# Input products of a recurrent layer: the seven-product scheme over 14 instead of 12 of 16 K tiles, with another plan for the weight sums and another order of products

## The chip, the cores and the metric

One core of one Trainium2 chip. The time is the device time of one launch in microseconds (us). TensorE multiplies; VectorE, ScalarE and GpSimd work elementwise; SyncE only issues DMAs here. In profiles they are PE (and PEld, its weight loads), DVE, ACT, POOL and SP.

## What is computed

The reference is one step of a two-layer trunk over 640 tokens of width 2048: 512 tokens of a prompt and 8 sequences of 16 tokens. The first layer is recurrent, the second is attention. The part that the change touches is the input side of the recurrent layer:

```python
def recurrent_mixer(hn, h0, conv0, w_in, conv_w, conv_b, w_r, b_r, w_i, b_i, lam, w_out):
    xb, zg = jnp.split(hn @ w_in, 2, axis=-1)
    xb, conv_new = causal_conv(xb, conv0, conv_w, conv_b)
    y, hT = rg_lru(xb, h0, w_r, b_r, w_i, b_i, lam)
    return (y * jax.nn.silu(zg)) @ w_out, hT, conv_new
```

`hn` is the normed input (640 x 2048), `w_in` is 2048 x 8192. Half of the 8192 outputs are features `xb`, half are gates `zg`. `rg_lru` makes two sigmoid gates from `xb` by small block products, then exp, tanh and sqrt, and scans over the tokens.

## The kernel before

**Layout.** Features lie on partitions, tokens along the free axis. The inner dimension of 2048 is 16 K tiles of 128, the outputs are 64 feature tiles of 128, and the 640 tokens are two halves of 320. Everything is float32 by way of three matmuls: operands are split into a high part in float32r and a low rest, and `mm3` (L99) adds high by high, high by low and low by high. So a weight tile that came by DMA is split first: `hilo` (L82) writes the high part on ScalarE (L87, tile wh) and the rest on VectorE (L88, tile wl).

**The stages.** A start stage norms the input, makes the conditioning vectors and already does the first four feature tiles (two of `xb`, two of `zg`, the list EARLY). The recurrent stage does the other 60 feature tiles as 30 pairs. Then come the output product of the layer, the shared keys and values, attention and its output product.

**A pair product** (`pair_product`, L543) makes two feature tiles for both halves of the tokens: a 2x2 block of results. For 12 of the 16 K tiles, taken as NP = 6 pairs, it uses a scheme that needs seven products instead of eight: sums of the input halves (the slots X11, X12, X22, S1 to S4 of the tiles xs) are made once in the start stage (`combine`, L403), and sums of weight quarters are made per pair of feature tiles. Each product is NP x 3 matmuls of 128x128 by 128x320. The other four K tiles (PLAIN, tiles xv) are done directly. Four banks hold partial results: a, b, c and d (pa, pb, pc, pd). Between products ScalarE copies bank a or c to SBUF (`keep`, L567), and VectorE combines a bank with a kept copy into the result (the evac functions, L637 and L682). TensorE goes on adding into the bank after the copy has read it, so a product that goes on in a bank waits for that bank's keep.

**The weights of a pair** come in nine slots, one for each of the seven products and two plain ones. `plan` (L441) and `pair_weights` (L499) are generators that write the loads, sums and splits in a fixed order; `ahead` (L535) keeps up to WB = 4 split slots ready. A sum of weight quarters is built by DMA: SyncE loads one quarter into a tile (`big_load`, L477), and GpSimd issues a second DMA which adds another quarter to it (`add`, L481). Six tiles rotate: r11 and r2 hold raw quarters, t1, t2, t3 and u2 hold sums. Each pair takes six loads and five additions of 384 KB, and two plain loads of 256 KB.

**Order around the products.** For `j` from 0 to 15 the recurrent stage does `silu_gates` (a pair product for `zg`, its evac into tiles zs, a sigmoid sg of it), `lru` (L691: gate blocks psg of 48 matmuls, their sigmoids g and q, then exp, tanh and sqrt on ScalarE, the scan on VectorE, and the results to DRAM tensor yd), and `inputs` and `conv` for the next pair of `xb`. ScalarE loads another function table ahead of the first sigmoid, the first exp and the first sqrt of each `j`. The scheduler of the tile framework sets the order on each engine from this program; each engine then works in order, and an instruction that waits holds up what stands behind it. `conv_rows` (L601) prepares the row buffers hb of the convolution: a memset and a copy of three columns per sequence (L609, L610), on GpSimd, after a small load pv.

In a steady period, from one gate block to the next, TensorE does 48 gate matmuls and two pair products of 174, in all 396.

## Time and profile before

| | |
|---|---|
| median of 3 runs | 2928.18 us (2927.59 to 2935.82) |
| the profiled execution | 2928.68 us |
| its span in the trace | 2927.0 us |
| TensorE busy | 2845.4 us, 97% |
| VectorE / ScalarE / GpSimd busy | 67% / 55% / 15% |
| start stage | 0 to about 144 us |
| recurrent stage, first to last pair product | about 144 to 1049 us |
| loads and additions of w_in_a quarters, median from issue to landing | 5.3 us (r), 3.6 us (t) / 6.4 us (t) |

The span is the time from the first to the last recorded instruction; the rest of the execution's time lies around it. In the rows of the timeline, columns are start in us, duration in us, engine, line, operation, output and inputs, shape and count; in brackets stands the idle time ahead of it and what ended it. In the groups, a row gives the count, the total busy time, the mean of one in ns, and after the second bar the idle time ahead of them. A matmul's duration includes its way through the array; matmuls that follow each other start about 147 ns apart while one lasts about 309 ns.

### The profile page before, as it was taken

Reading aid. Unit: us, or ns where it says so; the run is one execution under the profiler, and the core shown is the slowest. Engines: PE = TensorE matmul, PEld = TensorE weight load, DVE = VectorE, ACT = ScalarE, POOL = GpSimd, SP = SyncE. Lnnn points to the kernel's source line nnn. Section 1 sums busy time; section 2 is a strip of 40 time slices with the busy share of each in tenths; the row PEclk is TensorE's granted clock in tenths of the full one; section 3 lists DMA queues with packets and bytes.
Section 4 is the critical chain, followed back from the end, with each engine's and each line's share of the span. In section 5 each row is a group of like instructions: output and inputs, shape, how many; then the busy total and the mean of one; then the engine's idle time right before and its main releaser. Section 6 shows DMA issues by size and latency. Waiting matters only on the chain.

```text
span 2927.0 us, 48683 instructions
## 1 busy us (share of the span) xinstructions
PE 2845.4 (97%) x18874; PEld 2532.5 (87%) x18874; DVE 1961.7 (67%) x2795; ACT 1608.0 (55%) x2459; POOL 437.5 (15%) x683
## 2 busy tenths in 40 slices
PE   6889999999999999999999999999999999999998
PEld 4689999999999987778878999878989999897787
DVE  7666776677667766724468877787666766667335
ACT  5456655665566556623456667674455555546323
POOL 0022222223222200001113332001100000001000
PEclk9999999999999999999999999999999999999999
DMA  9977787778777756555567666663665555656636
GB/s 333 330 164 167 184 194 195 177 182 195 191 183 181 170 163 211 171 138 171 176 223 259 217 212 215 206 195 111 193 192 171 181 176 181 200 169 190 209 106 225
DMA packets 263287, 564.07 MB, mean 193 GB/s; under 512 B 24440, under 2 KB 108536, under 8 KB 261904
## 3 DMA queue, kind: packets, MB, share of 16 engines
q1 hardware_dynamic: 232016, 465.60, 50.1%
q0 software_dynamic: 31040, 95.36, 15.7%
q8 instruction: 148, 2.42, 0.3%
q14 instruction: 83, 0.68, 0.1%
HBM read 523.76 MB, written 37.11 MB: 192 GB/s over the span
## 4 chain that ended last, share of the span: by engine, by line
PE 85%; DMA 6%; ACT 4%; DVE 4%; issue 1%; POOL 0%; SPq 0%; DVEq 0%; POOLq 0%; ACTq 0%
PE acc L101 7%; PE acc L102 7%; PE acc L103 7%; PE psh L101 6%; PE acck L101 5%; PE psh L103 5%; PE psh L102 5%; PE acck L102 5%; PE acck L103 5%; PE pa L101 3%; PE pa L102 3%; PE pa L103 3%; PE pc L102 2%; PE pc L103 2%; PE pc L101 2%; DMA wa<-w_ada_dram 2%
## 5 line engine op out<-in xcount | busy, mean ns | idle before, releaser
L88 DVE TENSOR_TENSOR wl<-wr,wh 128x1024 fp32r<-128x1024 f32 x216 | 270.5, 1254 | 285.4 <-ACT wh L87 282.2
L87 ACT ACTIVATE wh<-wr 128x1024 fp32r<-128x1024 f32 x216 | 228.1, 1056 | 379.6 <-PE acc L103 221.7
L101 PE MATMUL acc<-wh,yh 128*128 128x512 f32 x960 | 379.4, 396 | 9.8 <-ACT yh L785 5.4
L102 PE MATMUL acc<-wl,yh 128*128 128x512 f32 x960 | 378.0, 394 | 5.7 <-DVE wl L88 5.6
L103 PE MATMUL acc<-wh,yl 128*128 128x512 f32 x960 | 375.3, 393 | 0.8 <-DVE yl L786 0.8
L186 DVE TENSOR_TENSOR wa<-wa,wa 128x1024 bf16<-128x1024 f32 (+1 forms) x256 | 313.6, 1260 | 23.0 <-ACT wa L185 20.9
L101 PE MATMUL psh<-nh,wh 128*128 128x320 f32 x1024 | 323.9, 316 | 0.0
L103 PE MATMUL psh<-nh,wl 128*128 128x320 f32 x1024 | 318.8, 311 | 0.0
L102 PE MATMUL psh<-nl,wh 128*128 128x320 f32 x1024 | 317.4, 310 | 0.0
L185 ACT ACTIVATE wa<-wa 128x1024 bf16<-128x1024 f32 x256 | 263.6, 1052 | 67.5 <-DVE wa L186 52.8
L101 PEld LDWEIGHTS acc<-wh,yh 128*128 128x128 f32 x960 | 182.1, 190 | 58.1 <-issue 8.7
L102 PEld LDWEIGHTS acc<-wl,yh 128*128 128x128 f32 x960 | 182.3, 190 | 45.7 <-DVE wl L88 8.4
L103 PEld LDWEIGHTS acc<-wh,yl 128*128 128x128 f32 x960 | 182.0, 190 | 39.8 <-DVE yl L786 2.1
L101 PEld LDWEIGHTS psh<-nh,wh 128*128 128x128 f32 x1024 | 192.3, 188 | 19.3 <-DVE ql L1120 12.6
L103 PEld LDWEIGHTS psh<-nh,wl 128*128 128x128 f32 x1024 | 192.4, 188 | 0.5 <-DVE wl L88 0.2
L102 PEld LDWEIGHTS psh<-nl,wh 128*128 128x128 f32 x1024 | 192.4, 188 | 0.1
L101 PE MATMUL pa<-xs,wh 128*128 128x320 f32 x540 | 171.8, 318 | 19.7 <-ACT keep L567 14.2
L481 POOL DMA_DIRECT2D t<-w_in_a_dram x105 | 93.5, 891 | 622.6 <-DMA t<-w_in_a_dram 465.1
L102 PE MATMUL pa<-xs,wh 128*128 128x320 f32 x540 | 168.3, 312 | 0.0
L103 PE MATMUL pa<-xs,wl 128*128 128x320 f32 x540 | 168.1, 311 | 0.0
L101 PE MATMUL acck<-nh,wh 128*128 128x320 f32 x512 | 161.5, 315 | 0.0
L103 PE MATMUL acck<-nh,wl 128*128 128x320 f32 x512 | 158.2, 309 | 0.0
(353 smaller groups left out, 7436.5 us busy)
## 6 DMA issues: line engine op xcount, KB each, us to landing
wa<-w_ada_dram SPq DMA_DIRECT2D x192, 512.0 KB, 4.7
wr<-w_out_a_dram SPq DMA_DIRECT2D x96, 512.0 KB, 4.3
t<-w_in_a_dram POOLq DMA_DIRECT2D x105, 384.0 KB, 6.4
r<-w_in_a_dram SPq DMA_DIRECT2D x90, 384.0 KB, 5.3
wr<-w_in_b_dram SPq DMA_DIRECT2D x64, 512.0 KB, 5.4
ck<-cache_k_dram SPq DMA_DIRECT2D x64, 512.0 KB, 6.5
cv<-cache_v_dram SPq DMA_DIRECT2D x64, 512.0 KB, 5.3
t<-w_in_a_dram SPq DMA_DIRECT2D x75, 384.0 KB, 3.6
```

The lines of the kernel that those rows point to most:

```text
L87: nc.scalar.activation(hi[:, :n], raw, AF.Copy)
L88: nc.vector.tensor_tensor(lo[:, :n], raw, hi[:, :n].bitcast(F32), ALU.subtract)
L101: mm(out, sh, mh, start=start, stop=False, **kw)
L102: mm(out, sh, ml, start=False, stop=False, **kw)
L103: mm(out, sl, mh, start=False, stop=stop, **kw)
L185: nc.scalar.activation(parts[i], raw, AF.Copy)
L186: nc.vector.tensor_tensor(parts[2] if i else raw, raw, parts[i], ALU.subtract)
L481: self.nc.gpsimd.dma_start(self.big[tag], self.quarter(w, i), accum_op=ALU.add)
```

## The change

- **NP goes from 6 to 7.** A product has 21 matmuls instead of 18, the plain part has two K tiles instead of four: 147 + 24 = 171 matmuls for a pair instead of 174. Split tiles are 128x896 instead of 128x768, plain slots 128x256 instead of 128x512.
- **The weight sums are chains.** A sum tile (sum0 and sum1 in turn) serves three slots of a pair: it is split, a quarter is added, it is split again, another is added, it is split a third time. Beside it are raw (two slots, plain loads), rest (a load, and an addition between its two slots) and one plain load for both plain slots. That makes four loads and four additions of 448 KB and one load of 256 KB for a pair. In the start stage one addition falls away, and the tiles that the early weights borrow are others.
- **Another order of products.** Before: X11, S1, S2, X12, plain b, S3, X22, plain d, S4, plain c, plain a. Now: S1, X11, S4, plain b and d, S2, X12, S3, plain c and a, X22. The copy of S1 gets a buffer of its own (keep5), the others have two instead of three. The result of bank a is taken before X22, that of bank d is the last.
- **The ring of split weights** has three buffers instead of four.
- **The row buffers** are prepared by VectorE instead of GpSimd.
- In the start stage there is a seventh pair to combine, and the input tiles are divided among other buffers.

```diff
--- before.py
+++ after.py
@@ -34,7 +34,7 @@
 NHEAD = 16
 PAST = 512
-NP = 6
+NP = 7
 PLAIN = range(2 * NP, KD)
 WQ = NP * P
@@ -300,7 +300,7 @@
         V.memset(self.ones, 1.0)
         acc = rp.tile([P, T], F32, tag="row", name="ssum", bufs=4)
-        homes = [("A", 7, (0, 1, 2, 3, 4, 5)), ("A", 7, (6, 7)), ("A", 7, (8, 9)), ("V", 2, (10, 12)), ("V", 2, (11, 13)), ("V", 2, (14,)), ("V", 2, (15,))]
+        homes = [("A", 7, (0, 1, 2, 3, 4, 5)), ("A", 7, (6, 7)), ("A", 7, (8, 9)), ("A", 7, (10, 11)), ("V", 2, (12, 14)), ("V", 2, (13, 15))]
         xs = [None] * KD
         for tag, n, ks in homes:
             x = self.ap.tile([P, n, T], F32, tag=tag, name=f"x{tag}", bufs=self.ABUFS[tag])
@@ -346,7 +346,7 @@
         spare = [self.zeroed(self.bank(n)) for n in ("psb", "pss")]
         units, wt = [], {}
-        tags = [t for t in self.BIG if t not in ("t2", "u2")]
+        tags = ("rest", 1), ("raw", 1), ("rv", 3), ("rv", 3)
         self.big = {}
         def fill(k):
@@ -362,9 +362,9 @@
                 with self.tc.issue_after(last):
                     r = self.spread(rp, rs)
             if k == 9:
-                self.big_load("t2", self.I["w_in_a"][1], 2)
-            if k in (11, 13):
-                self.add("t2", self.I["w_in_a"][1], (13 - k) // 2)
+                self.big_load("sum0", self.I["w_in_a"][1], 1)
+            if k == 11:
+                self.add("sum0", self.I["w_in_a"][1], 0)
             if k < 2 * NP:
                 if k % 2 == 0:
                     slot = self.ap.tile([P, 2, 7 * HALF], F32R, tag="A", name="xs", bufs=self.ABUFS["A"])
@@ -389,7 +389,8 @@
                     if k == 1:
                         units = self.first_units()
                     fill(k - 1)
-            raw = self.wp.tile([P, WQ], F32, tag=tags[(k - KD) % len(tags)], name="wf", bufs=1)[:, :512]
+            tag, bufs = tags[(k - KD) % len(tags)]
+            raw = self.wp.tile([P, 512 if tag == "rv" else WQ], F32, tag=tag, name="wf", bufs=bufs)[:, :512]
             nc.sync.dma_start(raw, self.I["w_first"][:, 4 * P * k : 4 * P * k + 4 * P])
             wt[k] = self.hilo(raw, P)
             if k % 2 == 0:
@@ -444,7 +445,7 @@
         order = [1] + [q for j in range(1, 16) for q in (16 + j, j + 1)][:-1]
         small = []
         for q in order:
-            small += [(w[q][:, 4 * WQ + i : 4 * WQ + i + WV], None) for i in (0, WV)]
+            small.append((w[q][:, 4 * WQ : 4 * WQ + 2 * WV], None))
             if q == 1 or q > 16:
                 small += [(x[0, max(0, q - 16)].rearrange("(k p) n -> p k n", p=P), 256) for x in g]
         self.small = iter(small)
@@ -452,19 +453,18 @@
         for _ in range(3):
             self.small_load()
         at = [w[q] for q in order] + [None, None]
-        for tag, n in (("r11", 0), ("t1", 1), ("r2", 3), ("t3", 1), ("u2", 2)):
-            self.big_load(tag, at[tag == "u2"], n)
-        for tag, n in (("t1", 0), ("t3", 2), ("u2", 1)):
-            self.add(tag, at[tag == "u2"], n)
+        for tag, n in (("raw", 0), ("rest", 2), ("sum1", 1)):
+            self.big_load(tag, at[tag == "sum1"], n)
         for i, q in enumerate(order):
-            yield from self.pair_weights(*at[i : i + 3], *("t2", "u2", "t2")[i % 2 : i % 2 + 2])
+            yield from self.pair_weights(*at[i : i + 3], *("sum0", "sum1", "sum0")[i % 2 : i % 2 + 2])
             if q == 1 or q > 16:
                 for _ in g:
-                    yield self.small_split(256)
-    BIG = "r11", "t1", "t2", "r2", "t3", "u2"
+                    x = self.urgent(self.smalls.pop(0), 256)
+                    self.small_load()
+                    yield x
     def quarter(self, w, i):
         return w[:, WQ * i : WQ * i + WQ]
@@ -472,7 +472,7 @@
     def big_load(self, tag, w, i):
         if w is not None:
-            pool = self.ep if tag == "u2" else self.wp
+            pool = self.ep if tag == "sum1" else self.wp
             self.big[tag] = pool.tile([P, WQ], F32, tag=tag, name=tag, bufs=1)
             self.nc.sync.dma_start(self.big[tag], self.quarter(w, i))
@@ -483,7 +483,7 @@
     def small_load(self):
         for src, width in islice(self.small, 1):
             raw = self.wp.tile([P, 512], F32, tag="rv", name="rv", bufs=3)
-            n = WV if width is None else 512
+            n = 2 * WV if width is None else 512
             self.nc.sync.dma_start(raw[:, :n] if width is None else raw.rearrange("p (a n) -> p a n", n=width), src)
             self.smalls.append(raw[:, :n])
@@ -491,45 +491,39 @@
         with self.tc.high_priority(200):
             return self.hilo(raw, width)
-    def small_split(self, width):
-        x = self.urgent(self.smalls.pop(0), width)
-        self.small_load()
-        return x
-    def pair_weights(self, w, after, later, t2, other):
+    def pair_weights(self, w, after, later, total, other):
         load, add = self.big_load, self.add
         split = lambda tag: self.urgent(self.big[tag], P)
-        x = split("r11")
-        load("r11", after, 0)
+        x = split(total)
+        add(total, w, 2)
         yield x
-        x = split("t1")
-        load("t1", after, 1)
+        x = split("raw")
+        load("raw", w, 3)
         yield x
-        x = split(t2)
-        add(t2, w, 3)
+        x = split("rest")
+        add("rest", w, 1)
         yield x
-        x = split("r2")
-        load("r2", w, 2)
-        add("t1", after, 0)
-        yield x
-        x = self.small_split(P)
+        plain = self.smalls.pop(0)
+        x = self.urgent(plain[:, :WV], P)
         add(other, after, 0)
         yield x
-        x = split("t3")
-        load("t3", after, 1)
+        x = split(total)
+        add(total, w, 3)
         yield x
-        x = split(t2)
-        load(t2, later, 2)
+        x = split("raw")
+        load("raw", after, 0)
         yield x
-        x = split("r2")
-        load("r2", after, 3)
-        add("t3", after, 2)
+        x = split("rest")
+        load("rest", after, 2)
         yield x
-        x = self.small_split(P)
-        add(t2, later, 1)
+        x = self.urgent(plain[:, WV:], P)
+        self.small_load()
+        yield x
+        x = split(total)
+        load(total, later, 1)
         yield x
     def ahead(self, held=0):
@@ -556,58 +550,56 @@
                 self.mm3(ps, hi[:, n, :], lo[:, n, :], x[:, 0, c], x[:, 1, c], first and n == 0, n == NP - 1, **kw)
             self.ahead()
-        def plain(ps, w, half):
+        def plain(ps, w, half, first):
             c = slice(HALF * half, HALF * half + HALF)
             for n, k in enumerate(PLAIN):
                 mh, ml = self.hT[k]
-                self.mm3(ps, w[0][:, n, :], w[1][:, n, :], mh[:, c], ml[:, c], False, k == KD - 1, **kw)
-        def keep(ps):
-            t = ep.tile([P, HALF], F32, tag="keep", name="keep", bufs=3)
+                self.mm3(ps, w[0][:, n, :], w[1][:, n, :], mh[:, c], ml[:, c], first and n == 0, k == KD - 1, **kw)
+        def keep(ps, tag="keep", bufs=2):
+            t = ep.tile([P, HALF], F32, tag=tag, name=tag, bufs=bufs)
             nc.scalar.activation(t, ps, AF.Copy)
             return t
-        a, c = bank("pa7"), bank("pc7")
+        c, a = bank("pc7"), bank("pa7")
+        seven(c, S1, True)
+        p5 = keep(c, "keep5", 1)
         seven(a, X11, True)
         p1 = keep(a)
-        seven(c, S1, True)
-        p5 = keep(c)
+        seven(c, S4, False)
+        b, d = bank("pb7"), bank("pd7")
+        w = self.weights()
+        plain(b, w, 0, True)
+        plain(d, w, 1, True)
+        self.ahead()
         seven(a, S2, False)
         u2 = keep(a)
-        b = bank("pb7")
-        seven(b, X12, True)
-        w = self.weights()
-        plain(b, w, 0)
+        seven(b, X12, False)
         evac(0, 0, b, p1, ALU.subtract)
-        d = bank("pd7")
-        plain_d = lambda: plain(d, w, 1)
         seven(a, S3, False)
         u3 = keep(a)
-        seven(d, X22, True)
-        plain_d()
-        self.ahead()
-        evac(0, 1, d, u3, ALU.subtract)
-        seven(c, S4, False)
         w = self.weights()
-        plain(c, w, 0)
+        plain(c, w, 0, False)
         evac(1, 0, c, u2, ALU.add)
-        plain(a, w, 1)
+        plain(a, w, 1, False)
         self.ahead()
         evac(1, 1, a, p5, ALU.add)
+        seven(d, X22, False)
+        evac(0, 1, d, u3, ALU.subtract)
     HW = 3 + TP + NB * (TS + 3)
     S0 = 3 + TP
     def conv_rows(self, j, ep):
-        G = self.nc.gpsimd
+        V = self.nc.vector
         pv = ep.tile([P, 2, 40], F32, tag="pv", name="pv", bufs=2)
         self.nc.sync.dma_start(pv, self.I["lru"][:, 2 * j : 2 * j + 2, :])
         rows = []
         for h in range(2):
             hb = ep.tile([P, self.HW + 1], F32, tag="hb", name="hb", bufs=2)
-            G.memset(hb[:, 0:3], 0.0)
-            G.tensor_copy(hb[:, self.S0 : self.HW].rearrange("p (b t) -> p b t", t=TS + 3)[:, :, 0:3], pv[:, h, 8:32].rearrange("p (b t) -> p b t", t=3))
+            V.memset(hb[:, 0:3], 0.0)
+            V.tensor_copy(hb[:, self.S0 : self.HW].rearrange("p (b t) -> p b t", t=TS + 3)[:, :, 0:3], pv[:, h, 8:32].rearrange("p (b t) -> p b t", t=3))
             rows.append(hb)
         return pv, rows
@@ -1371,7 +1363,7 @@
             self.od = dp.tile([D, T], F32, name="od")
             self.constants()
             self.pp = E(self.pool("ps", space=PSUM))
-            self.WB, self.WW = 4, WQ
+            self.WB, self.WW = 3, WQ
             with self.pool("A") as self.ap, self.pool("w7") as self.wp:
                 self.h0t = self.mp.tile([P, NB], F32, name="h0t")
                 self.k4, self.nk8 = (self.mp.tile([P, FT], F32, name=n) for n in ("k4", "nk8"))
```

What the scheduler makes of it is seen in the order of instructions on an engine. On GpSimd, from the end of the start stage to the first convolution, there stood before (t and u are tiles of weight sums, hb the row buffers, st the states for the output):

```order
L481 DMA t_1548<-w_in_a_dram 128x768
L609 MEMSET hb 128x3 x2
L652 COPY st<-hb 128x3
L653 COPY st<-hb 128x24
L652 COPY st<-hb 128x3
L653 COPY st<-hb 128x24
L481 DMA u_1533<-w_in_a_dram 128x768
L610 COPY hb<-pv 128x8x3 x2
L481 DMA u_1533<-w_in_a_dram 128x768
```

Now there stands:

```order
L481 DMA rest<-w_in_a_dram 128x896
L644 COPY st<-hb 128x3
L645 COPY st<-hb 128x24
L644 COPY st<-hb 128x3
L645 COPY st<-hb 128x24
L481 DMA sum_1543<-w_in_a_dram 128x896
L481 DMA sum_952<-w_in_a_dram 128x896
```

The copies into hb have gone from between two additions to VectorE's queue.

On ScalarE, at a gate block in the middle of the stage (sg is the sigmoid of a pair product's result, g and q the gates), before:

```order
L687 ACT_TABLE_LOAD
L687 ACTIVATE sg<-zs 128x640
L87 ACTIVATE wh<-r_5194 128x768
L87 ACTIVATE wh<-t_5220 128x768
L687 ACTIVATE sg<-zs 128x640
L710 ACTIVATE g<-psg_5576,pv 128x320
L710 ACTIVATE g<-psg_5584,pv 128x320
L710 ACTIVATE q<-psg_5593,pv 128x320
```

and now:

```order
L87 ACTIVATE wh<-sum_5742 128x896
L679 ACT_TABLE_LOAD
L679 ACTIVATE sg<-zs 128x640
L702 ACTIVATE g<-psg_6096,pv 128x320
L702 ACTIVATE g<-psg_6104,pv 128x320
L702 ACTIVATE q<-psg_6113,pv 128x320
L679 ACTIVATE sg<-zs 128x640
L702 ACTIVATE q<-psg_6121,pv 128x320
```

Before, the table load and the first sg stood two weight splits ahead of the gates; now a weight split stands ahead of the table load, and the gates follow right behind the first sg.

Also on ScalarE, from the exp of a period to the second product of the next pair, before:

```order
L720 ACT_TABLE_LOAD
L720 ACTIVATE q<-g,nk_100 128x640
L87 ACTIVATE wh<-rv 128x512
L720 ACTIVATE q<-g,nk_100 128x640
L724 ACTIVATE g<-g,k_99 128x640 x2
L87 ACTIVATE wh<-t_4713 128x768
L732 ACT_TABLE_LOAD
L732 ACTIVATE g<-g 128x640
L87 ACTIVATE wh<-t_4461 128x768
L732 ACTIVATE g<-g 128x640
L567 ACTIVATE keep<-pa_5044 128x320
L738 ACTIVATE q<-q,mone 128x640
```

and now:

```order
L712 ACT_TABLE_LOAD
L712 ACTIVATE q<-g,nk_100 128x640
L87 ACTIVATE wh<-rv 128x256
L712 ACTIVATE q<-g,nk_100 128x640
L716 ACTIVATE g<-g,k_99 128x640 x2
L561 ACTIVATE keep_5611<-pc_5583 128x320
L87 ACTIVATE wh<-sum_5102 128x896
L724 ACT_TABLE_LOAD
L724 ACTIVATE g<-g 128x640 x2
L87 ACTIVATE wh<-raw 128x896
L730 ACTIVATE q<-q,mone 128x640
L87 ACTIVATE wh<-rest 128x896
```

The first keep (of bank c, keep5) stands now behind tanh instead of the first keep (of bank a) behind sqrt, and the split of the raw quarter (for X12) stands behind both sqrt.

On TensorE the scheduler also moves some matmuls: in the first pair product after a gate block, three plain matmuls of bank b stand between X11 and S4, and X12 begins ahead of S2.

## The prediction

> **What bounds the kernel now.** I read the page first.
>
> ```profile
> PE 2845.4 (97%) x18874; PEld 2532.5 (87%) x18874; DVE 1961.7 (67%) x2795; ACT 1608.0 (55%) x2459; POOL 437.5 (15%) x683
> ```
>
> TensorE is busy for 97% of the span, so time is to be won in two ways only: fewer matmuls, or less waiting of TensorE. The recurrent stage is the one that the change touches, so I cut it with the table of windows where the start-up of that stage ends and the steady periods begin (columns: length, busy time of PE, PEld, DVE, ACT, POOL, the granted clock, the DMA share, GB/s).
>
> ```profile
> 144.00:282.00 138.00, 123.64 (x793) 121.50 (x794) 92.19 (x148) 77.43 (x122) 30.95 (x64) 0.95 0.71 169
> 282.00:1049.00 767.00, 761.54 (x5150) 754.93 (x5149) 551.28 (x831) 463.24 (x688) 182.99 (x316) 1.00 0.75 181
> ```
>
> The steady part has 5150 matmuls, 13 periods of 396, so a period is 767 / 13 = 59.0 us. The first part loses 14 us of TensorE, and its granted clock is lower. Next come the waits of TensorE in the whole stage, and then in its steady part alone (engine, tile, line, what it waited for: sum, times, longest).
>
> ```profile
> PE pa L101 <- ACT keep L567: 18.1, 17, 6.2
> PE pa L101 <- ACT hb L632: 5.5, 1, 5.5
> ```
>
> ```profile
> PE pa L101 <- ACT keep L567: 5.0, 13, 0.4
> ```
>
> So in the steady part TensorE waits once a period, 0.4 us, for a keep; the rest, 13.1 + 5.5 us, is lost in the first 138 us. The timeline of TensorE there shows two of these waits and what follows them.
>
> ```profile
> 138.44 0.28 PE L103 MATMUL pss<-xv,wl 128*128 128x256 f32 x1
> 144.22 0.64 PE L101 MATMUL pa<-xs,wh 128*128 128x320 f32 x1 [5.50 <-ACT hb L632]
> ...
> 148.69 0.31 PE L101 MATMUL pc<-xs,wh 128*128 128x320 f32 x1
> ...
> 151.18 0.31 PE L103 MATMUL pc<-xs,wl 128*128 128x320 f32 x1
> 157.66 0.64 PE L101 MATMUL pa<-xs,wh 128*128 128x320 f32 x1 [6.18 <-ACT keep L567]
> ...
> 162.22 0.31 PE L101 MATMUL pb<-xs,wh 128*128 128x320 f32 x1
> ```
>
> From 148.69 to 151.18 there are 17 steps in 2.49 us: a matmul costs 0.1465 us. The 18 from 144.22 to 148.69, behind the long wait, took 4.47 instead of 2.64 us, and the 31 from 157.66 to 162.22 are as slow at their start: each long wait costs some 1.85 us more afterwards, and the granted clock of the window tells the same. What held ScalarE, which both waits name:
>
> ```profile
> 141.48 1.58 ACT L87 ACTIVATE wh<-t 128x768 fp32r<-128x768 f32 x2 [4.33 <-DMA t<-w_in_a_dram]
> ...
> 143.70 0.47 ACT L632 ACTIVATE hb<-psb 128x384 f32<-128x384 f32 x1
> ...
> 155.83 0.94 ACT L657 ACTIVATE ca<-hb,pv 128x664 f32<-128x664 f32 x1 [9.31 <-POOL hb L610]
> ```
>
> ```profile
> 154.73 0.86 POOL L481 DMA_DIRECT2D u<-w_in_a_dram  x1 [5.98 <-DMA u<-w_in_a_dram]
> 155.26 0.66 POOL L610 COPY hb<-pv 128x24 f32<-128x24 f32 x2
> ```
>
> ```profile
> 145.94 1.40 SPq L605 DMA_DIRECT2D pv<-lru_dram  x2
> ```
>
> ```profile
> DMA to landing us min/median/max: 8.7/8.8/9.0
> ```
>
> First ScalarE waits for a weight sum whose addition lands late, and the copies that free the banks stand behind that split. Then it waits for the row buffers, whose copies stand on GpSimd behind an addition that itself waits for a load; and the small load pv that they read was there no earlier, 9 us after its issue (the last two rows: SyncE's queue, and the landing of the two pv loads in this stretch).
>
> **The change, part by part.** The sum is made against the profiled execution's 2928.68 us (span 2927.0 us); the median of the runs, 2928.18 us, is 0.5 us below it.
>
> *Matmuls.* 30 pairs lose 3 each: 90 x 0.1465 = -13.2 us. All are on the path, as TensorE is. Beside this 0.1465 us: the Trainium skill (TensorE: Matmul & The Clock Gate, Part 2, the back-to-back issue gap) gives N / 2.4 + 2.5 ns for a warm array, 136 ns at N = 320, by which the term would be an estimated -12.2 us; the trace has 8% more, and it decides.
>
> *Start-up.* The new first split is of a raw quarter, and the sum tile begun in the start stage gets its addition earlier, with one addition fewer ahead of it: ScalarE has no late sum to wait for. But the raw split (estimated at 0.95 us on ScalarE and 1.1 us on VectorE, below) stands ahead of the last norm copy, so I move the last early matmul from 138.44 to about 140.2; with a bank copy (0.47 us) behind it the first product starts at about 141.2 instead of 144.22: -3.0 us, and -1.8 us as the remaining gap of 1 us is near the short steady waits, which show no slow matmuls. The second wait nearly goes: 157.66 - 151.18 - 0.15 = 6.3 us and 1.9 us of slow matmuls are 8.2 us. GpSimd's addition no longer holds the copies into hb, which stand on VectorE. What is late next is pv: in the new order SyncE issues it behind a load that waits for the last norm copy, 24 early matmuls ahead of 140.2, so near 136.7. With 8.8 us it lands at 145.5; the copies (0.66), the convolution's first step (0.94), a small split and keep5 (0.41 each) end near 147.9, and S4 wants keep5 at 141.2 + 42 x 0.1465 = 147.4. With the 4.7 us that a pv load takes in the median of the whole run, nothing is left. I leave 0.5 us: -7.7 us. Two more waits of the start-up remain to be judged:
>
> ```profile
> 215.28 0.49 DVE L682 TENSOR_TENSOR zs<-pb,keep 128x320 f32<-128x320 f32 x1 [5.19 <-DMA yd<-zs]
> ```
>
> ```profile
> 216.35 0.64 PE L101 MATMUL pa<-xv,wh 128*128 128x320 f32 x1 [3.97 <-ACT keep L567]
> ```
>
> ```profile
> 268.56 0.42 PE L101 MATMUL pa<-xs,wh 128*128 128x320 f32 x1 [2.75 <-ACT keep L567]
> ```
>
> The first two belong together: VectorE may not write zs before its two buffers have been written out to yd, and this transfer comes from the first gate block, which moves forward with everything else. I keep it whole: 0. The third hangs on the split of an added tile; with one addition at a time in each tile I take -1.5 us, between 0 and -2.4 us (2.75 less the steady 0.4). Start-up: -3.0 - 1.8 - 7.7 - 1.5 = -14.0 us, between -17 and -8.
>
> *Steady periods.* Splits of new sizes are not in the trace; the nearest rows are
>
> ```profile
> L87 ACT ACTIVATE wh<-t 128x768 fp32r<-128x768 f32 x90 | 75.6, 841 | 81.7 <-PE pa L102 37.9 <-issue 24.5 <-PE pd L102 12.7
> L87 ACT ACTIVATE wh<-wr 128x1024 fp32r<-128x1024 f32 x216 | 228.1, 1056 | 379.6 <-PE acc L103 221.7 <-PE psh L102 120.2 <-DMA wr<-w_out_b_dram 15.5
> L88 DVE TENSOR_TENSOR wl<-t,wh 128x768 fp32r<-128x768 f32 x90 | 85.8, 954 | 26.2 <-ACT wh L87 26.1
> L88 DVE TENSOR_TENSOR wl<-wr,wh 128x1024 fp32r<-128x1024 f32 x216 | 270.5, 1254 | 285.4 <-ACT wh L87 282.2
> ```
>
> Half way between them, 128x896 takes 0.95 us on ScalarE and 1.10 us on VectorE. Now one period of ScalarE, with the gate block that begins at 576.71 on TensorE:
>
> ```profile
> 576.71 0.31 PE L101 MATMUL psg<-xh,wh 128*128 128x320 f32 x1
> ...
> 594.41 0.42 PE L101 MATMUL pa<-xs,wh 128*128 128x320 f32 x1 [0.39 <-ACT keep L567]
> ```
>
> ```profile
> 571.25 1.28 ACT L687 ACT_TABLE_LOAD   x1
> ...
> 577.57 0.72 ACT L687 ACTIVATE sg<-zs 128x640 f32<-128x640 f32 x1
> ...
> 584.55 0.51 ACT L710 ACTIVATE q<-psg,pv 128x320 f32<-128x320 f32 x1
> 585.08 1.28 ACT L720 ACT_TABLE_LOAD   x1
> 586.38 0.83 ACT L720 ACTIVATE q<-g,nk 128x640 f32<-128x640 f32 x1
> ...
> 588.36 1.54 ACT L724 ACTIVATE g<-g,k 128x640 f32<-128x640 f32 x2
> ...
> 593.94 0.41 ACT L567 ACTIVATE keep<-pa 128x320 f32<-128x320 f32 x1
> ```
>
> Before, the table load came 5.5 us ahead of the gate block, and the last gate was done 8.35 us after its start. With X22 last, sg waits for the last result; a split and the load come after the start of the block. From 0.1 us on ScalarE has a split (0.85 from start to start), the load 1.3, two sg 1.4, eight gates 3.8 and two more splits 1.8: the last gate is done at 9.2 us. Then follow table load 1.30, exp 0.73, a small split 0.42, exp 0.73, two tanh 1.44 and keep5 0.41 (steps between starts in these rows): keep5 ends 14.2 us after the block began. TensorE wants it for S4 after 48 + 42 + 3 matmuls, at 93 x 0.1465 = 13.6 us: a wait of 0.6 us with its restart. Behind keep5 ScalarE has a sum split, the table load and two sqrt until about 17.75 us, then the raw split 0.95, and VectorE its rest 1.1: 19.8 us. TensorE, at S4 from 14.2, wants this rest for the third matmul of X12, 21 + 9 + 2 matmuls later, at 18.9: 1.0 us with the restart 1.1. Keeps of bank a ahead of S3 and the plain parts add 0.3. Together 2.0 us a period, where the trace has 767 - 5150 x 0.1465 = 12.5 us in 13 periods, 0.96 each: +1.05 x 13 = +13.7 us. The bounds: 0.96 as now (0 us), if the gates keep their time; 3.5 (+33 us), if one more split of 0.95 and one sigmoid stand ahead of the gates. I take 2.0, built from the rows' own steps. On the table loads a rule speaks against the change: the Trainium skill (ScalarE: Activation LUTs, What ACT_TABLE_LOAD costs) puts a drain of 1.38 us on top of each load's 1.28 us. In the rows above exp starts 0.02 us after its load ends, so this trace shows no such drain; by the page the load now behind the block's start would make the wait for keep5 an estimated 1.4 us longer, and the time an estimated 18 us.
>
> *Additions.* A sum tile goes through split, addition and split again in four slots: three products and the plain part, 3 x 21 x 0.1465 + 12 x 0.1465 = 11.0 us.
>
> ```profile
> t<-w_in_a_dram POOLq DMA_DIRECT2D x105, 384.0 KB, 6.4
> ```
>
> 6.4 us by 7/6 is 7.5 us; with 0.95 and 1.1 us of splits the loop takes 9.5 us. That holds, with 1.5 us to spare and what three ring buffers hold ahead: 0.
>
> *Exit.* The first output product begins with the last gate block; ScalarE's first yh split stood among the gates, and now stands behind the last tanh.
>
> ```profile
> 1048.95 0.30 PE L101 MATMUL psg<-xh,wh 128*128 128x320 f32 x1
> ...
> 1055.99 0.40 PE L101 MATMUL acc<-wh,yh 128*128 128x512 f32 x1
> ...
> 1065.49 0.50 PE L101 MATMUL acc<-wh,yh 128*128 128x512 f32 x1 [2.49 <-ACT yh L785]
> ```
>
> Gates to 7.9 (48 x 0.1465, the array's way of 0.3, a sigmoid of 0.51), table load, two exp, two tanh and a split of 0.73 give 12.9 us after 1048.95, where it began after 7.04: +5.9 us and some 2 us of slow matmuls; the wait of 2.49 us and the slow matmuls behind it go: +3.5 us, between 0 and +6.
>
> The sum: -13.2 - 14.0 + 13.7 + 3.5 = -10.0 us, so 2918.7 us by the profiled execution and 2918.2 us by the median. I forecast 2918.4 us, between the two.
>
> **The rivals.** *The waits of a period don't grow.* If X12's raw quarter is split before exp begins, the 13.7 us fall away: 2928.7 - 23.7 = 2905 us. For it speaks that VectorE and ScalarE are idle for over a quarter of the steady window (551 and 463 of 767 us); against it, that both work in order, and the order puts that split behind both sqrt.
>
> *pv comes late.* If SyncE issues pv behind the raw split's rest, near 141, it lands at 150 and keep5 ends at 152: S4 waits 4.6 us and 1.85 us of slow matmuls follow. Of the 7.7 us 1.7 are left: -13.2 - 8.0 + 13.7 + 3.5 = -4.0 us, about 2924.7 us, no change. For it speaks that pv is issued behind two loads of 448 KB, as it was behind two or three of 384 KB; against it, that the new start moves less: 5 loads and additions of 448 KB where there were 11 of 384 KB.
>
> *ScalarE paces the period (slower).* In the gate block eight half blocks share four banks, so the fifth, 24 matmuls or 3.5 us after the start, needs the first sigmoid done. By my working it ends at 3.5 us: sum split 0.85, table load 1.3, sg 0.65, sigmoid 0.5, after 0.1. If the last result or the sum comes 1.5 us later, gates, exp, keep5 and the raw split all come later by that, and TensorE, which waits for this chain at each of those places, has a period longer by 1.5: waits of 3.5 us, -13.2 - 14.0 + 33 + 3.5 = +9.3 us, about 2938 us. It decides from where the waits pass 0.96 + (13.2 + 14.0 - 3.5) / 13 = 2.8 us a period. For it speaks that there is no slack at the fifth half block. Against it: the last result is read by VectorE, which in the steady window is idle for 216 of 767 us.
>
> **How the numbers follow.** A measurement of this kernel can tell 0.3%, 8.8 us, from no change; that is 2919.4 us and 2937.0 us. The forecast gets 0.44; its own range is 2912 to 2925, and 0.27 lies below 2919.4. The first rival gets 0.21 (all faster), the second 0.17 (all within), the third 0.18, of it 0.10 beyond 2937.0 and 0.08 within. So faster 0.48, within 0.17 + 0.17 + 0.08 = 0.42, slower 0.10. The range, 2903 to 2935, holds the forecast, the second rival and most of the first; it leaves out 0.08 of the first below it and 0.12 of the third above.
>
> **What would show it.** Right: 18,784 matmuls (18,874 less 90); a first gate block near 166 us (141.2 + 171 x 0.1465), with at most a short wait at the first S4; a steady period of 59 us with waits of pc for a keep (0.6 us) and of pb for wl (1.1 us); the first acc some 13 us after the last gate block begins. Wrong: a period near 58 us (first rival) or 60.5 us (third), a wait of 4 us or more at the first S4 (second), or waits of wh for additions.

## The result and the profile after

The changed kernel takes 2910.38 us (median of 4 runs, 2907.38 to 2916.01), the kernel before 2928.36 us: a ratio of 0.9933, with a 95% interval of 0.9921 to 0.9946. That is 18 us, where 10 were forecast. The traced execution of the changed kernel is the longest of the four (2916.01 us, span 2914.3), so its trace shows only 12.7 of the 18 us; a second trace of the same kernel (below) shows 15.6. The time lies in the range on record, 2903 to 2935 us, but below the forecast's own 2912 to 2925, and nearer to the first rival's 2905 than to 2918.4.

The page and three windows of the trace after (columns as before: length, busy time of PE, PEld, DVE, ACT, POOL, granted clock, DMA share, GB/s):

```profile
PE 2837.1 (97%) x18784; PEld 2520.8 (86%) x18784; DVE 1977.9 (68%) x2867; ACT 1607.8 (55%) x2464; POOL 420.3 (14%) x589
```

```profile
120.00:149.00 29.00, 24.66 (x168) 21.13 (x167) 17.91 (x57) 11.95 (x20) 0.88 (x1) 0.82 0.76 241
...
149.00:269.00 120.00, 116.40 (x778) 114.16 (x779) 93.74 (x162) 76.18 (x120) 24.87 (x42) 1.00 0.64 148
...
269.39:1033.58 764.19, 753.03 (x5072) 743.86 (x5071) 565.54 (x880) 462.59 (x690) 169.97 (x245) 1.00 0.66 153
```

There are 90 matmuls fewer, as counted. The steady part from gate block 3 to the last is 764.19 us; the kernel before has 767.09 there. The stretch up to gate block 3 was to lose waits, and did; but the 29 us that end at the first product ran at a granted clock of 0.82. TensorE's timeline gives the marks by which I cut both traces: the first product, gate blocks 1 and 3, the last gate block. First the two marks of the kernel before that the prediction doesn't show, then those of the changed kernel.

```profile
179.82 0.31 PE L101 MATMUL psg<-xh,wh 128*128 128x320 f32 x1
...
281.86 0.31 PE L101 MATMUL psg<-xh,wh 128*128 128x320 f32 x1
```

```profile
149.79 0.41 PE L101 MATMUL pc<-xs,wh 128*128 128x320 f32 x1 [1.30 <-ACT hb L624]
...
175.11 0.31 PE L101 MATMUL psg<-xh,wh 128*128 128x320 f32 x1
...
269.39 0.31 PE L101 MATMUL psg<-xh,wh 128*128 128x320 f32 x1
...
1033.58 0.31 PE L101 MATMUL psg<-xh,wh 128*128 128x320 f32 x1
```

| stretch | before, us | after, us | difference | forecast |
|---|---|---|---|---|
| to the first product | 144.22 | 149.79 | +5.6 | -3.0 |
| first product to gate block 1 | 35.60 | 25.32 | -10.3 | -9.9 |
| gate block 1 to 3 | 102.04 | 94.28 | -7.8 | -2.8 |
| gate block 3 to the last (13 periods) | 767.09 | 764.19 | -2.9 | +2.3 |
| last gate block to the end of the span | 1878.04 | 1880.72 | +2.7 | +3.5 |
| sum | 2927.0 | 2914.3 | -12.7 | -10.0 |

(The forecast's 90 matmuls are put in the stretch where they fall: 0.4, 1.3 and 11.4 us.) The sum was near in part by luck: three of its terms missed, by +8.6, -5.0 and -5.2 us, and the misses cancel for the most part.

**The steady period.** TensorE's waits from gate block 3 to the last, after:

```profile
PE pb L103 <- DVE wl L88: 11.2, 13, 0.9
```

Of the forecast's two waits one came, X12's, and with the price given to it. In one period, with the gate block at 504.52, it reads (TensorE, ScalarE, VectorE):

```profile
504.52 0.31 PE L101 MATMUL psg<-xh,wh 128*128 128x320 f32 x1
...
522.87 0.31 PE L102 MATMUL pb<-xs,wh 128*128 128x320 f32 x1
524.03 0.42 PE L103 MATMUL pb<-xs,wl 128*128 128x320 f32 x1 [0.85 <-DVE wl L88]
```

```profile
504.58 0.95 ACT L87 ACTIVATE wh<-sum 128x896 fp32r<-128x896 f32 x1 [2.25 <-PE pd L102]
505.55 1.28 ACT L679 ACT_TABLE_LOAD   x1
...
512.67 0.56 ACT L702 ACTIVATE q<-psg,pv 128x320 f32<-128x320 f32 x1
513.25 1.28 ACT L712 ACT_TABLE_LOAD   x1
...
517.75 0.42 ACT L561 ACTIVATE keep<-pc 128x320 f32<-128x320 f32 x1
...
520.32 1.37 ACT L724 ACTIVATE g<-g 128x640 f32<-128x640 f32 x2
521.59 0.94 ACT L87 ACTIVATE wh<-raw 128x896 fp32r<-128x896 f32 x1
```

```profile
522.90 1.08 DVE L88 TENSOR_TENSOR wl<-raw,wh 128x896 fp32r<-128x896 f32 x1
```

The raw split stands behind both sqrt and ends at 522.5, its rest follows 0.4 us later and ends 19.5 us after the gate block began (19.8 in the forecast); TensorE's third matmul of X12 wanted it at 523.0. keep5 ended 13.65 us after the start of the block (14.2 in the forecast), just when S4 wanted it (13.6): no wait. A period has 390 matmuls, 57.14 us, and 1.65 us of waits and restarts; before it had 396, 58.01 us, and 0.99.

**The queue of GpSimd.** The wait of 3.97 us that I had kept whole is gone. GpSimd's rows at the first transfer to yd, before and after:

```profile
207.90 0.88 POOL L481 DMA_DIRECT2D u<-w_in_a_dram  x1 [3.44 <-DMA u<-w_in_a_dram]
208.44 0.92 POOL L748 DMA_DIRECT2D yd<-zs  x1
```

```profile
201.10 0.59 POOL L740 DMA_DIRECT2D yd<-zs  x1 [0.25 <-DVE zs L739]
```

Before, yd's issue stood behind an addition that waited 3.44 us for a load; the data were ready at 205.7. After, it was issued as soon as the data were there. This is the place that the forecast missed: it looked at who waits for the transfer and not at what holds its issue.

### The profile page after: what moved, and what is told of

Its sections match the earlier page's. It is cut to its first block, busy times and chain, and to the rows that moved or that the text cites. A ratio compares the mean times of both kernels' runs of the same rounds, so it can differ in the third digit from the quotient of the medians.

```text
span 2914.3 us, 48223 instructions
## 1 busy us (share of the span) xinstructions
PE 2837.1 (97%) x18784; PEld 2520.8 (86%) x18784; DVE 1977.9 (68%) x2867; ACT 1607.8 (55%) x2464; POOL 420.3 (14%) x589
## 4 chain that ended last, share of the span: by engine, by line
PE 79%; ACT 6%; DVE 4%; DMA 2%; issue 2%; POOL 0%; DVEq 0%; POOLq 0%; SPq 0%; ACTq 0%
PE acc L101 7%; PE acc L102 7%; PE acc L103 7%; PE psh L101 6%; PE acck L101 5%; PE psh L103 5%; PE psh L102 5%; PE acck L103 5%; PE acck L102 5%; PE pa L101 3%; PE pa L103 3%; PE pa L102 3%; PE psa L198 2%; DVE wl L88 1%; PE pc L101 1%
## 5 line engine op out<-in xcount | busy, mean ns | idle before, releaser
L101 PE MATMUL acc<-wh,yh 128*128 128x512 f32 x960 | 378.8, 395 | 10.3 <-ACT yh L777 5.6
L102 PEld LDWEIGHTS acc<-wl,yh 128*128 128x128 f32 x960 | 182.5, 190 | 47.7 <-DVE wl L88 10.3
L101 PE MATMUL pa<-xs,wh 128*128 128x320 f32 x630 | 194.8, 309 | 0.0
L103 PE MATMUL pa<-xs,wl 128*128 128x320 f32 x630 | 194.7, 309 | 0.0
L102 PE MATMUL pa<-xs,wh 128*128 128x320 f32 x630 | 194.7, 309 | 0.0
L481 POOL DMA_DIRECT2D sum<-w_in_a_dram x90 | 79.4, 882 | 559.3 <-DVE wl L88 262.9
```

What stands on the lines that cost most here:

```text
L101: mm(out, sh, mh, start=start, stop=False, **kw)
L102: mm(out, sh, ml, start=False, stop=False, **kw)
L103: mm(out, sl, mh, start=False, stop=stop, **kw)
L481: self.nc.gpsimd.dma_start(self.big[tag], self.quarter(w, i), accum_op=ALU.add)
```

## The experiments

Two theories. **Queue theory:** the gain lies ahead of gate block 3, where fewer additions hold GpSimd's queue, and a steady period wins 0.2 us only, as X12's wait takes what the matmuls give. **Matmul theory:** the gain is that of 90 matmuls, 13.2 us. All runs are timed against the kernel before on the same chip; ratios have 95% intervals. The median of the kernel before was 2928.4 to 2931.9 us on the chips used, so the ratios compare two runs better than their medians do.

| run | median, us | ratio to before | gate block 1 | gate block 3 | 13 periods | from the last gate block to the end |
|---|---|---|---|---|---|---|
| e1 | 2911.92 | 0.9926 (0.9911 to 0.9941) | 173.15 | 267.44 | 764.24 | 1879.7 |
| e2 | 2927.87 | 0.9990 (0.9979 to 1.0001) | 166.29 | 268.02 | 777.68 | 1879.3 |
| e3 | 2911.56 | 0.9928 (0.9913 to 0.9942) | 171.34 | 267.23 | 764.05 | 1877.8 |
| e4 | 2896.09 | 0.9880 (0.9861 to 0.9899) | 169.44 | 263.76 | 749.87 | 1881.1 |
| e5 | 2923.31 | 0.9964 (0.9952 to 0.9976) | 176.75 | 272.98 | 767.17 | 1880.5 |
| e6 | 2930.26 | 0.9994 (0.9982 to 1.0006) | 177.02 | 281.42 | 767.25 | 1873.9 |
| e7 | 2926.12 | 0.9985 (0.9970 to 0.9999) | 181.63 | 281.12 | 770.34 | 1873.6 |
| e8 | 2891.20 | 0.9862 (0.9840 to 0.9883) | 172.33 | 266.60 | 749.55 | 1872.3 |
| e9 | 2901.20 | 0.9905 (0.9889 to 0.9922) | 167.34 | 262.10 | 755.09 | 1879.9 |
| e10 | 2890.07 | 0.9867 (0.9848 to 0.9887) | 167.72 | 262.01 | 749.83 | 1873.0 |
| e11 | 2892.15 | 0.9873 (0.9860 to 0.9885) | 173.67 | 267.99 | 749.81 | 1874.4 |
| e12 | 2924.78 | 0.9983 (0.9974 to 0.9991) | 176.14 | 281.24 | 769.66 | 1878.3 |

**e1, the changed kernel again.** No edit.

> The changed kernel unedited, for a second trace and more times. Queue theory (the gain sits ahead of the third gate block, where GpSimd's additions held the copies into hb and the transfers to yd; a steady period wins only 0.2 us): 0.9925 to 0.9955 of the kernel before; gate block 3 begins near 265 to 270 us (281.86 before), the steady period is 58.78 us again, and the slow matmuls from 125 to 148 us of the first trace, with a granted clock of 0.85 there, need not come again; without them the first gate block begins near 168 us instead of 175.11. Matmul theory (the gain is that of 90 matmuls, 13.2 us): the same ratio, but then the steady period is shorter by 0.88 us.

0.9926, a period of 58.79 us, gate block 3 at 267.44: the queue theory's numbers. The stretch from 120 to 148 us had a granted clock of 0.94 instead of 0.82, and gate block 1 came 2 us sooner, at 173.15, but not at 168: something besides the clock may be late there (e10). The last column of the table needs care: the kernel before, e5, e6, e7 and e12 have the same exit and 1873.6 to 1880.5 us there, so only means over several runs say something.

**e2, NP = 6 in the new order.**

```diff
-NP = 7
+NP = 6
```

(with the input tiles divided as before and the plain load's tile twice as wide.)

> The changed kernel with NP = 6: the new plan, chains and order of products with 12 K tiles in the scheme, 90 matmuls more. Queue theory: the start-up gain stays, and the period is 396 x 0.1465 = 58.0 us and waits of 0.6 to 1.4 us, so 59 us and a little: about 2918 to 2922 us, some 8 to 12 us above the changed kernel and still 6 to 10 us under the kernel before. Matmul theory: back to the kernel before, 2926 us or more.

The time is the matmul theory's, 2927.87 us, but not for its reason. Gate block 3 stays at 268.02, so the start-up gain does not hang on the matmuls; what takes it back is the steady part, where TensorE's waits read

```profile
PE pb L101 <- ACT wh L87: 18.7, 13, 1.4
```

and 13 periods take 777.68 us: 754.2 of matmuls and 1.81 us of waits a period. I had put 0.6 to 1.4. The new plan and order by themselves cost 0.8 us a period against those before; the seventh pair takes back 1.03 us, 0.88 of it matmuls. Neither theory stands alone: up to gate block 3 the start gives 13.8 us (281.86 - 268.02), the new plan and order cost 10.6 (777.68 - 767.09), and NP = 7 gives 13.4 back (777.68 - 764.24).

**e3, the row buffers back on GpSimd.**

```diff
-        V = self.nc.vector
+        G = self.nc.gpsimd
...
```

> The changed kernel with the row buffers prepared by GpSimd as before. If moving the copies to VectorE brought the start-up gain: the first S4 waits again for keep5 behind the copies, 4 us and more with slow matmuls after it, so +5 to +8 us. If it is the fewer additions in the start that brought it: the copies stand behind one addition that has its data, and the time stays within 1.5 us of the changed kernel.

Nothing changes (2911.56 against 2911.92 us). GpSimd's rows:

```profile
148.38 1.12 POOL L481 DMA_DIRECT2D sum<-w_in_a_dram  x1
148.92 0.92 POOL L602 COPY hb<-pv 128x24 f32<-128x24 f32 x2
```

The copies stand behind one addition, and neither waits. So it was not the move to VectorE. That an addition in GpSimd's queue held something up is shown for yd (e5); that the copies gained by the fewer additions is only argued.

**e4, the keeps ahead.** The scheduler had put X12 ahead of S2, since the copy of bank a stood late on ScalarE.

```diff
-            nc.scalar.activation(t, ps, AF.Copy)
+            with self.tc.high_priority(200):
+                nc.scalar.activation(t, ps, AF.Copy)
```

> The changed kernel with the keep copies emitted at the scheduler's high priority, so that ScalarE makes the copies of banks c and a ahead of the tanh and sqrt work and TensorE does S2 ahead of X12. If the steady wait of 1.02 us (X12's third matmul for the rest of the raw quarter) comes from X12 standing ahead of S2: it goes, the period falls to 57.5 to 57.9 us, and the time by 11 to 17 us to 2893 to 2899 us. Rival: ScalarE's chain itself is late, and the wait moves to the gates or to the next split: a period of 58.3 us or more, at most 6 us gained.

2896.09 us, 15.8 us under e1 (14.4 of it in the steady part of the two traces), and the steady part from gate block 3 to the last reads

```profile
263.76:1013.63 749.87, 749.87 (x5073) 743.92 (x5071) 563.78 (x880) 462.48 (x690) 147.49 (x245) 1.00 0.67 155
```

PE busy equals the window: no wait is left, 57.68 us a period. So the wait was made by the order of X12 and S2, as ScalarE's total work is the same (462.5 us).

**e5, before, with yd issued by SyncE.**

```diff
-            G.dma_start(self.yd[P * f : P * f + P, :], zs[h])
+            self.nc.sync.dma_start(self.yd[P * f : P * f + P, :], zs[h])
```

> The kernel before with one edit: the transfers to yd are issued by SyncE and no longer by GpSimd. Queue theory: the wait of 3.97 us at 216.35 and the slow matmuls behind it come from the transfer's issue standing behind an addition that waits for its load (issued at 208.44, the data of it ready at 205.7); on SyncE it goes at once: the third gate block begins 4 to 6 us earlier than 281.86, and the steady periods stay at 58.97 us: 4 to 6 us faster in all. Rival: the transfer itself is slow there because the DMA engines are full, and the wait stays: within 1.5 us of the kernel before, or slower if SyncE's loads now wait behind it.

```profile
202.70 0.33 SPq L748 DMA_DIRECT2D yd<-zs  x1
```

Gate blocks 1 to 3 take 96.2 instead of 102.0 us: the wait of 3.97 us and its slow matmuls are gone, 5.8 us less in all. That is a net figure: the wait of 2.75 us at 268.56, the third in the prediction, went too, and a new one came,

```profile
215.68 0.71 PE L101 MATMUL psg<-xh,wh 128*128 128x320 f32 x3 [2.68 <-ACT xh L666]
```

The queue theory holds at this place. The ratio of 0.9964 says 10 us, where 4 to 6 were expected; in the trace 3 us more lie ahead of gate block 1, for which I have no cause (in e6 and e7, which have the same start stage, gate block 1 began at 177.0 and 181.6, so the start alone moves by that much).

**e6, before, with the row buffers on VectorE.**

```diff
-        G = self.nc.gpsimd
+        V = self.nc.vector
...
```

> The kernel before with one edit: the row buffers are prepared by VectorE, as in the changed kernel. If GpSimd's addition held the copies into hb (my step): the wait of 6.18 us at 157.66 shrinks by the 0.5 us from pv's landing (154.92) to the copies' end only, unless pv lands sooner. If pv's landing sets it (which the run with the rows on GpSimd in the changed kernel suggests): the same, within 1.5 us of the kernel before. A gain of 5 us or more would speak for the step as the prediction had it.

No gain: the copies now wait for pv itself.

```profile
153.05 0.26 DVE L610 COPY hb<-pv 128x24 f32<-128x24 f32 x2 [7.92 <-DMA pv<-lru_dram]
```

**e7, before, with the keeps ahead.** The same edit as e4, in the kernel before.

> The kernel before with the keep copies at high priority, nothing else. If the order of products of the kernel before has little to lose there: its steady wait of 0.55 us a period (S2 for the keep of bank a behind sqrt) goes and the period falls from 58.97 to 58.3 to 58.5 us: 6 to 9 us faster. Together with the run of the changed kernel with this edit (57.68 us a period) it says what the change is worth where the keeps are not late: 0.6 to 0.9 us a period, the matmuls' 0.88 and no more. Rival: the edit helps only the new order, and the period stays at 58.9 us or grows.

2926.12 us, where 6 to 9 us less had been expected; the 13 periods take 3.2 us more than in the kernel before and become uneven (58.26 to 62.06 us). One wait in them is 3.5 us long:

```profile
PE pa L101 <- ACT keep L568: 10.5, 10, 3.5
```

The edit helps the steady periods only in the new order. The rival holds; what makes the periods uneven stays open.

**e8, e4 with the exit's first splits ahead.** The first split of wr and the first two of yh get the same priority.

```diff
+            if len(ys) < 2 and len(chunks) == 4:
+                with self.tc.high_priority(200):
+                    split()
...
```

> The changed kernel with the keep copies and the first splits of the output product (one of wr, two of yh) at high priority. If the exit's loss comes from yh standing behind the last tanh: the first output matmul begins 7 to 8 us after the last gate block's start instead of 12.8, and of the 5.6 us 3 to 5 remain in the end: 2890 to 2893 us. Rival: the gates are held up by these splits, or the next yh is late by the same amount: 2895 us or more.

2891.20 us. In the changed kernel TensorE's first output matmul stood 12.8 us after the last gate block,

```profile
1046.35 0.79 PE L101 MATMUL acc<-wh,yh 128*128 128x512 f32 x1 [5.57 <-ACT yh L777]
```

now it starts at 1021.42, 5.3 us after 1016.15, among the last gates. From the last gate block to the end, e8, e10 and e11 have 1873.2 us in the mean; the two traces of the changed kernel, e3 and e4, which have its exit, 1879.8; and the five with the exit of the kernel before 1876.9. So the new exit cost 2.9 us by these means (the five scatter by 6.8 us, so this size is rough), and the edit wins 6.6; by the medians e8 is 4.9 us under e4. With both edits the kernel takes 0.9862 of the kernel before.

**e9, NP = 6 with the keeps ahead.** The edits of e2 and e4.

> The changed kernel with NP = 6 and the keep copies at high priority: against the run with NP = 7 and this edit (57.68 us a period, 2896.1 us) it prices the 90 matmuls where neither has the steady wait. If a wait was what swallowed their gain: a period of 58.4 to 58.7 us, 0.75 to 1.0 us above 57.68, and over the steady part +10 to +13 us; the start gives back some (first gate block near 167 us), so 2903 to 2909 us. Rival: TensorE was not the bound and the 90 matmuls are worth little: a period within 0.4 us of 57.68.

2901.20 us, 5.1 above e4. The steady part:

```profile
262.10:1017.19 755.09, 755.09 (x5151) 755.04 (x5149) 557.28 (x880) 455.60 (x690) 158.72 (x245) 1.00 0.63 145
```

58.08 us a period, of which 58.01 are matmuls: at NP = 6 nothing is lost. At NP = 7 (e4) it is 57.68, of which 57.14 are matmuls; 0.54 us a period goes, most of it in four gaps of about 0.1 us that no wait in the trace explains. So the 78 matmuls of the steady part bring 0.40 us a period, 5.2 us, and not their 11.4: the rival's figure (within 0.4) was nearer than mine. What takes the other half stays open.

**e10, the first split behind the last norm copy.** ScalarE's rows in the changed kernel, where the first product was late:

```profile
128.70 0.74 ACT L384 ACTIVATE xv<-hn 128x640 fp32r<-128x640 f32 x1 [0.40 <-DVE hn L383]
...
141.23 0.95 ACT L87 ACTIVATE wh<-raw 128x896 fp32r<-128x896 f32 x1 [3.42 <-PE pss L102]
142.09 0.72 ACT L384 ACTIVATE xv<-hn 128x640 fp32r<-128x640 f32 x1
```

The raw split waits 3.42 us for one of three ring buffers, and the last norm copy stands behind it. Part of that wait is the slow clock: TensorE's matmuls, which free the buffer, ran at a granted clock of 0.50 from 134.05 to 140.88. In e4, where the clock was 1.00, the same wait is a third:

```profile
136.07 0.95 ACT L87 ACTIVATE wh<-raw 128x896 fp32r<-128x896 f32 x1 [1.15 <-PE pss L102]
```

The edit, on e8:

```diff
+        if not self.ready:
+            return self.hilo(raw, width)
         with self.tc.high_priority(200):
```

> The kernel with keep, wr and yh splits at high priority (2891.2 us), and the very first weight split (the raw quarter) without the high priority, so that on ScalarE it stands behind the last norm copy and no longer ahead of it. In the changed kernel it waits there 3.4 us for one of three ring buffers, and the last norm copy behind it comes at 137 to 142 us, 9 to 13 us after the one before, where it was 7.2 us in the kernel before. If this is what ate the start's gain: the last norm copy comes 7 to 8 us after the one before, the first product starts 3 to 6 us earlier, near 139 to 141 us, and the time is 2885 to 2888 us. Rival: the last loads of the conditioning weights set the start: no change beyond 1.5 us.

The last norm copy comes 6.7 us after the one before (13.4 above), and the first product at 137.40. Not all of that is the edit: the copy ahead of the last one came at 124.62 us here, at 129.40 in e8 and at 131.01 in e11, which has the same edit and its first product at 144.58. What the order does is seen in the distance of the two copies: 9.1 to 13.4 us in the five traces with the raw split between them (the changed kernel, e1, e3, e4, e8; 10.1 and 9.1 in e4 and e8, where the clock there was 1.00), 6.7 to 8.0 in five without (before, e2, e9, e10, e11). But of the time nothing comes that can be told from noise: 2890.07 us, 1.1 under e8, where 2885 to 2888 was expected, and the ratios are 0.9867 and 0.9862. The gate block still needs 30.3 us behind the first product (26.2 in e8). ScalarE waits again, for the copies:

```profile
142.84 0.94 ACT L652 ACTIVATE ca<-hb,pv 128x664 f32<-128x664 f32 x1 [3.12 <-DVE hb L605]
```

**e11, e10 with pv loaded early.**

```diff
             if k == 9:
+                self.pv0 = self.mp.tile([P, 2, 40], F32, name="pv0")
+                nc.sync.dma_start(self.pv0, self.I["lru"][:, 0:2, :])
...
```

> The run with the calm first split (2890.07 us), and the first pv load issued in the start stage, at the tenth K tile, into a tile of its own. There the first product started at 137.40 us, but the next ones waited for keeps that stood behind a 3.12 us wait for the copies into hb, and those for pv: the first gate block still came at 167.72, 30.3 us after the first product, where 25.1 us are work. If pv is what is late next (my second rival, come true only once the first product is early): the keeps no longer wait, the first gate block comes 25 to 27 us after the first product, near 163 to 165 us, and the time is 2885 to 2888 us. Rival: the plain weights or the sum are as late as pv: no change beyond 1.5 us.

pv was issued at 85.4 us and landed within 6.9 us, and the wait stayed: gate block 1 came 29.1 us after the first product (144.58), and the time is 2892.15 us, no gain. VectorE's rows show what it is:

```profile
145.19 0.18 DVE L168 TENSOR_TENSOR sp<-sp,sp 128x32 f32<-128x32 f32 x1
...
149.66 0.20 DVE L174 TENSOR_SCALAR nk<-sp 128x32 f32<-128x32 f32 x1
149.76 0.17 DVE L610 COPY hb<-pv 128x24 f32<-128x24 f32 x1
```

A chain of small instructions that makes the decay parameters, each waiting for the last, stands ahead of the copies in VectorE's queue. On GpSimd the copies would not stand behind it; moving the copies there together with e10 was not tried.

**e12, before, with both edits of the second wait.** Row buffers on VectorE (e6) and pv early (e11).

> The kernel before with the row buffers on VectorE and the first pv load issued in the start stage. The two edits together take away both things that could hold the copies into hb at 151 to 157 us: the addition ahead of them on GpSimd, and pv's landing. If pv and the addition were equally late (each edit alone brings nothing): the wait of 6.18 us at 157.66 goes down to 0 to 1.5 us, and with the slow matmuls behind it the second gate product starts 5 to 8 us earlier: 4 to 8 us under the kernel before, third gate block near 274 to 277 us. Rival: the split of the added tile t or u holds ScalarE there in any case: within 2 us of the kernel before.

TensorE's waits in the start-up of this run:

```profile
147.86 0.64 PE L101 MATMUL pa<-xs,wh 128*128 128x320 f32 x1 [6.73 <-ACT hb L637]
```

```profile
212.65 0.64 PE L101 MATMUL pa<-xv,wh 128*128 128x320 f32 x1 [3.96 <-ACT keep L569]
```

The wait at S2 is gone altogether: gate block 1 comes 28.3 us after the first product, where it took 35.6. So pv and the addition were about equally late, as the rows of the kernel before say too (the addition issued at 154.73, pv landed near 154.9), and either hid the other (pv early alone was not tried). The ratio is 0.9983 (0.9974 to 0.9991), 5 us; the yd wait is still there, as it must be. Gate block 3 did not come at 274 to 277 as expected, but at 281.24: in this trace, one of the longest of twelve, the first product was 3.6 us later than in the kernel before, and gate blocks 1 to 3 took 3.1 us more.

## Why the prediction was right, and where it was not

*Matmuls (-13.2 forecast).* The count holds, and so does the price of a step (755.09 us for 5148 matmuls in e9 are 0.1467 each). What it is worth was mis-sized: the 0.88 us a period is count times price, no measurement, and between e9 and e4, where neither has a wait, a period differs by 0.40 us. In the steady part that is 5.2 of the 11.4 us; the changed kernel with X12's wait had 13.4 us more than e2, but there the wait shrank as well.

*First product (-3.0 forecast, +5.6 found).* This step failed. I priced the raw split ahead of the last norm copy by its length, 0.95 + 1.1 us, and took TensorE's speed there as given. Both were short. The split has a wait of its own, for one of three ring buffers until TensorE frees it: 1.15 us in e4 and 1.14 in e8, where the clock was 1.00 at that place, 3.42 us here. "Every wait that a moved instruction carries" was the missing term. The larger part goes with the slow clock (last section): in e4, whose edit doesn't touch this stretch, the first product came at 143.10, 1.9 us behind the 141.2 of the forecast, and here 8.6. That a fourth ring buffer would have spared the wait was not run.

*The second wait (-9.5 to gate block 1 beside the matmuls, -9.9 found).* Right in size, half right in cause. From the first product to gate block 1 it is 25.32 us, for 171 matmuls at 0.1465 = 25.05: nothing is lost there. I had ascribed this to the copies' move to VectorE; e3 says that the move is worth nothing in the new plan, e6 that it is worth nothing in the old one as long as pv lands late, and e12 that pv and the addition have to go together. In the changed kernel pv isn't late because the first product is: it was issued at 144.45 and landed 5.6 us later at most, and the copies came at 152.34, right behind the decay chain, while S4 wanted keep5 near 156. Where e10 made the first product early, a wait came back, not for pv but for VectorE's queue. My second rival named the place and not the releaser. One count in the prediction is wrong: from 157.66 to 162.22 the trace has 18 matmuls, not 31. The 1.9 us of slow matmuls stands, as 18 steps take 4.56 us there instead of 2.64.

*The yd wait (0 forecast, -5.8 by e5, with its slow matmuls).* This step failed: "this transfer comes from the first gate block, which moves forward with everything else". The wait was not the transfer's length but its place in GpSimd's queue (e5). The third wait (-1.5 forecast) is gone too, 2.75 us in the kernel before; four small ones of 0.6 to 1.0 us stand between gate blocks 1 and 3 now, where there were two of 0.2 and 1.0 beside the long ones.

*Steady waits (2.0 us a period forecast, 1.65 found).* The mechanism and the place were right: X12's third matmul, for the rest of the raw quarter, behind both sqrt. The term that was mis-sized is keep5: the last gate came 8.7 us after the block's start and not 9.2, so S4 didn't wait. 13 x 0.35 us are 4.6 of the 5.2 us that the steady part came out better. The Trainium skill (ScalarE: Activation LUTs, What ACT_TABLE_LOAD costs) has a drain of 1.38 us with each table load; here again there is none: the load of 1.28 us begins at 513.25, and the next exp at 514.54. By the page keep5 would have come an estimated 1.4 us later for each load, and S4 would have waited.

*Exit (+3.5 forecast, +2.9 found in the means).* Right: the first output matmul came 12.8 us after the last gate block (12.9 forecast), and e8 shows the cause. The size is rough, for the scatter named there.

*The rivals.* The first was the right direction in part: one of two waits did not come. The third, ScalarE as the pace, did not come: e4 has the same work on ScalarE and no wait.

## What to carry to other kernels

An instruction that a change moves brings its own waits along: ask of a split or a copy that is put earlier which buffer it needs and who frees it, before its duration is counted. Where two releasers are late together, the trace names the later one only, and removing it alone shows nothing; remove both once (e12) before calling either innocent. And a saving in matmuls is worth what the order of the other engines leaves of it: here the priority of the bank copies (e4, 15.8 us) was worth more than the 90 matmuls (13.2 us by their count, 5.2 in the steady part where nothing waits).

## What the runs showed of the hardware that was not expected

The start of this kernel differs between runs by its clock. From 120 us to the first product, the windows of the changed kernel's second trace (e1) and of e4, where the first trace had 0.82:

```profile
120.00:148.00 28.00, 23.21 (x181) 19.05 (x182) 18.46 (x58) 13.66 (x25) 0.88 (x1) 0.94 0.84 273
```

```profile
120.00:143.00 23.00, 18.48 (x155) 14.41 (x153) 16.43 (x52) 12.10 (x21) 0.88 (x1) 1.00 0.82 261
```

The first product came at 149.79, 147.83 and 143.10, in the order of the clocks 0.82, 0.94 and 1.00. The clock is not all: in e11 it was 1.00 too, and the first product came at 144.58, as the norm copies ahead of it were later than in e4 (131.01 against 126.86 for the last but one). The ten runs of the changed kernel lie between 2906.60 and 2916.01 us. X12's wait of 0.85 us in each steady period leaves the clock at 1.00, and so do the waits of 2.75 us in the kernel before (268.56) and 2.68 in e5 (215.68); the waits of 4 to 6 us in the start-up before were each followed by slow matmuls. The Trainium skill (TensorE: Matmul & The Clock Gate, Part 1) lets the clock halve after about 3.4 us without work, in windows that run freely, so that one kernel meets it differently from run to run. The long waits agree with that. Ahead of the slow stretch in the first trace TensorE's gaps are 1.6 us at most, but there was little work in them:

```profile
130.64:134.05 3.41, 1.28 (x17) 0.39 (x17) 0.00 (x0) 0.00 (x0) 0.00 (x0) 1.00 0.99 317
134.05:140.88 6.83, 6.83 (x26) 6.83 (x27) 3.79 (x12) 2.46 (x4) 0.88 (x1) 0.50 0.40 141
```

TensorE, which waited for loads of wa, was busy for 1.28 of 3.41 us, and then the clock was 0.50 for 6.83 us. So short gaps can come before a slow stretch too. Where the limit lies these traces don't show: in e4 a window with 1.54 of 3.41 us (93.25 to 96.66) was not followed by one.
